# Attention steps of a hybrid decoder layer: value products issued in pairs, stride 1 ordered before stride 4, queries loaded four steps sooner

## The chip, the cores and the metric

The kernel runs on one core of one Trainium2 chip. The metric is the device time of one execution in microseconds, given as the median of several runs. TensorE is called PE here, VectorE DVE, ScalarE ACT, GpSimd POOL and SyncE SP, as in the profile. PE multiplies matrices, DVE and ACT work on rows in parallel, POOL does slower elementwise work, and nearly all DMA transfers of this kernel are issued by SP, one after the other in program order.

## What is computed

The layer projects 4096 prompt positions of width 1024 to queries, keys, values, an attention gate and a recurrent branch. Eight heads of width 64 evaluate three window patterns each: 128 keys back with stride 1, 4 and 16. Their outputs are merged by their softmax denominators, gated, joined with the recurrent branch and sent through one output projection with a layer norm. A short decode step (8 x 4 tokens) is computed beside it.

```python
DIL_PATTERNS = ((128, 1), (512, 4), (2048, 16))

def _dilated_prompt(q, k, v, d):          # one pattern, stride d
    l = s // d                            # d classes of l positions
    o, m, den = _band_attention(sub(q), sub(k), sub(v))   # window of 128 keys inside a class
    ...

def _merge(parts):
    m_max = jnp.max(jnp.stack([p[1] for p in parts]), axis=0)
    ws = [den * jnp.exp(m - m_max) for (_, m, den) in parts]
    total = sum(ws)
    return sum(w[..., None] * o for w, (o, _, _) in zip(ws, parts)) / total[..., None]

y_att = _merge([_dilated_prompt(qh, kh, vh, d) for _, d in DIL_PATTERNS])
```

## The kernel before

The kernel has four phases, one after the other. Phase 1 projects to queries, keys and values and writes them to scratch in HBM. Phase 2 is the attention of the prompt, and the change lies in it. Phases 3 and 4 are the recurrent branch, the decode step and the output projection.

**Units and steps.** Phase 2 runs through 8 units. A unit is one pair of heads (index `c`) and one half of the sequence (2048 positions, index `st`); units 0, 2, 4 and 7 have the first half, where part of the windows is empty and the step is smaller. A unit has 48 steps, so there are 384. A step handles 128 queries of two heads against 256 keys in one pattern (`pat` 0 is stride 16, 1 is stride 4, 2 is stride 1). Four steps (`b` = 0 to 3) form a group. In this kernel the groups of a unit come in the order (pattern, quarter): (1,0), (2,0), then the four groups of stride 16 on steps 8 to 23, then (1,1), (2,1), (1,2), (2,2), (1,3), (2,3). A quarter `nb` is 512 positions (`SPAN`).

**One step on the engines.** `front` (L510 on) issues four score products on PE (lines 515 and 516, tile `s`), adds the mask and takes the minimum on DVE (L522) and the exponential on ACT (L526). `middle` transposes the probabilities on PE (L535, tile `pt`) and copies them to SBUF (tile `pts`). `back` multiplies them with the values on PE (L551, tile `o`, two halves of 64 output partitions) and, at the last step of a group, copies the group's output to SBUF on ACT: tile `u16` for stride 16 (two buffers), tile `u1` for stride 4 (three buffers), tile `u2` for stride 1 (two). The loop at the end of phase 2 runs them as a pipeline: at step i it issues `front(i)`, then about four products of an independent gate projection (`feed`, tile `f`, lines 653 to 658), then `back(i-4)`, then `middle(i-2)`.

**Queries.** The queries of a unit lie in tile `QT`, in four quarters. Stride 1 reads them in place. For strides 4 and 16 POOL first gathers them (`gather_q`, L465, tile `qg`, four buffers), three steps ahead of the `front` that reads them. The stride 16 steps read all four quarters. A quarter of the next unit's queries is loaded (`load_Q`, L399, four transfers of 256 KB) two steps after the last step of that quarter.

**The merge.** When the last group of a quarter is done, at step L of the unit (L = 23, 31, 39, 47 for quarters 0 to 3), a chain of small pieces is put at fixed numbers of steps behind it: denominators out to HBM at L+3 and back at L+6, weights at L+11 and L+12 (store `wd<-wg`), `spread` at L+15 (two transfers `gb<-wd`, L607, 384 KB each), `combine` from L+17 and `store` at L+21 (`ad<-gb`, L623). `combine` is five POOL operations, the first at L620 and four at L798, one or two per step. All of it works in one tile `gb`, which has a single buffer, so `spread` of a quarter waits for `store` of the quarter before it. Quarter 2 of a unit is merged in steps 8 to 11 of the next unit and quarter 3 in steps 16 to 19.

**What sets the order.** Each engine and each queue works in program order. A POOL gather that stands behind an operation of `combine` in the program waits for it, and a transfer on SP that stands behind `store` waits until POOL has ended `combine`.

Of the kernel before, what the change touches and what calls it, by code (L numbers as in the profile page):

```python
# [8 lines left out]
F32 = mybir.dt.float32  # L9
# [14 lines left out]
SPAN = 512  # L24
# [6 lines left out]
class Kern:  # L31
# [373 lines left out]
    def phase2(self):  # L405
# [3 lines left out]
        def pool(name, bufs, space=None):  # L409
            return ctx.enter_context(tc.tile_pool(name=name, bufs=bufs, reuse_waits="tile", **({"space": space} if space else {})))  # L410
# [4 lines left out]
        up = pool("p2u", 3)  # L415
# [9 lines left out]
        KT, QT, Wg, load_K, load_Q = self.KT, self.QT, self.Wg, self.load_K, self.load_Q  # L425
# [26 lines left out]
        def defer(k, f, *a):  # L452
            later.setdefault(now[0] + k, []).append((f, a))
# [3 lines left out]
        def gather_q(x):  # L457
            x.q = qp.tile([128, 4, 128], F32R, tag="qg", name="qg")
            if x.pat:
                q = QT[:, x.a].rearrange("p h s (m r) -> p (h s) r m", r=4)[:, :, x.b]  # L460
                o = x.q
            else:
                q = QT.rearrange("p g h s (i r) -> p g (h s) r i", r=16)[:, :, :, 4 * x.a + x.b]
                o = x.q.rearrange("p k (g i) -> p g k i", g=4)
            nc.gpsimd.tensor_copy(o, q.bitcast(F32))  # L465
# [29 lines left out]
        def v_ap(c, st, pat, a, b, kb):  # L495
            g = st * 4 + a
            if pat == 0:
                return V16[c, st - 1 + kb, a][:, b]
            if pat == 1:
                return V4[c, g - 1 + kb][:, b]  # L500
            if kb:
                return V1[c, g][:, b]
            return V1[c, g][:, b - 1] if b else V1[c, g - 1][:, 3]
# [39 lines left out]
        def back(x):  # L543
            kbs = (0, 1) if x.full else (1,)
            if x.b == 0:
                x.grp.o = ps_o.tile([128, 512], F32, tag="o", name="o")
            o = x.grp.o
            for kb in kbs:
                v = v_ap(x.c, x.st, x.pat, x.a, x.b, kb)
                for h in range(2):  # L550
                    nc.tensor.matmul(o[h * 64:(h + 1) * 64, x.b * 128:(x.b + 1) * 128],  # L551
                                     v[:, h * 64:(h + 1) * 64], x.pt[:, h, kb],
                                     start=(kb == kbs[0]), stop=(kb == 1), skip_group_check=True)
            if x.b == 3:
                if x.pat == 0:
                    nc.scalar.copy(x.unit.u16.rearrange("p (i r) -> p r i", r=16)[:, 4 * x.a:4 * x.a + 4],
                                   o.rearrange("p (r i) -> p r i", r=4))
                else:
                    t = up.tile([128, SPAN], F32, tag=f"u{x.pat}", name="u", bufs=4 - x.pat)
                    if x.pat == 1:  # L560
                        nc.scalar.copy(t.rearrange("p (m r) -> p r m", r=4), o.rearrange("p (r m) -> p r m", r=4))
                    else:
                        nc.scalar.copy(t, o)
                    x.unit.u[x.pat, x.a] = t
# [46 lines left out]
        def combine(un, nb):  # L611
            s, gb = slice(nb * SPAN, (nb + 1) * SPAN), un.gb[nb]
            e = nc.gpsimd
            for k, (f, o, y) in enumerate(((e.tensor_mul, 0, un.u16[:, s]), (e.tensor_mul, 1, un.u[1, nb]),
                                           (e.tensor_mul, 2, un.u[2, nb]), (e.tensor_add, 0, gb[:, 1]),
                                           (e.tensor_add, 0, gb[:, 2]))):
                if k:
                    defer(min(k, 3), f, gb[:, o], gb[:, o], y)
                else:
                    f(gb[:, o], gb[:, o], y)  # L620
# [65 lines left out]
        def wx_stage(c):  # L686
            raw = wx[c] = (vp.tile([128, 512], F32, tag="v16", name="wst", bufs=4) if c < 4 else
                           vp.tile([128, 512], F32, tag=("v4", "v1")[c % 2], name="wst"))
            self.w_stage(raw, self.I["w_in"], DIN, 2048, c, True)
# [41 lines left out]
        units = []  # L731
        for i in range(8):
            un = S()
            un.i, un.c, un.st0, un.st, un.u, un.gb, un.w = i, i // 2, i % 2 if i < 6 else 7 - i, {}, {}, {}, {}
            units.append(un)
        steps = []
        for un in units:
            order = [(1, 0), (2, 0)] + [(0, w) for w in range(4)]
            for nb in range(1, 4):
                order += [(1, nb), (2, nb)]  # L740
            for pat, a in order:
                grp = S()
                for b in range(4):
                    x = S()
                    x.unit, x.c, x.st, x.pat, x.a, x.b, x.grp = un, un.c, un.st0, pat, a, b, grp
                    steps.append(x)

        def vload(i):
            x = steps[i]
            if x.b:  # L750
                return
            g = x.st * 4 + x.a
            if x.unit.i == 6 and x.a == 0 and x.pat:
                f = (load_V16, load_V4, load_V1)[x.pat]
                f(x.c, g - 1)
                return defer(5, f, x.c, g)
            if x.pat == 0:
                if x.st:
                    load_V16(x.c, 0, x.a)
                load_V16(x.c, x.st, x.a)  # L760
            elif x.pat == 1:
                load_V4(x.c, g)
            else:
                load_V1(x.c, g)

        vload(0)
        vload(4)
        for x in steps[:3]:
            gather_q(x)
        feed(self.f0[0])  # L770
        N, staged, split = len(steps), 0, 0
        for i in range(N + 26):
            now[0] = i
            if i < N:
                x = steps[i]
                un = x.unit
                if x.pat == 1 and x.a == 0 and x.b == 0:
                    un.u16 = u16p.tile([128, ST], F32, tag="u16", name="u16")
                    un.ac = sp.tile([128, 3, 16, 2, 2], F32, tag="ac", name="ac")
                    if un.i < 6 and un.st0 == 0:  # L780
                        defer(self.kl[0], load_K, un.c, 4, 2)
                        defer(self.kl[1], load_K, un.c, 6, 2)
                if x.pat and x.b == 0:
                    un.st[x.pat, x.a] = sp.tile([128, 4, 2, 2], F32, tag=f"st{x.pat}", name="st")
                x.stat = un.ac[:, 0, 4 * x.a + x.b] if x.pat == 0 else un.st[x.pat, x.a][:, x.b]
                front(x)
            feed(self.f0[i + 1] if i + 1 < len(self.f0) else self.fill_rate[x.unit.i] if i < N else 96)
            if 0 <= i - 4 < N:
                back(steps[i - 4])
            if 0 <= i - 2 < N:  # L790
                middle(steps[i - 2])
            if i + 3 < N and steps[i + 3].pat < 2:
                gather_q(steps[i + 3])
            for k in (1, 5):
                if i + k < N and (steps[i + k].pat == 0) == (k == 1):
                    vload(i + k)
            for f, a in later.pop(i, []):
                f(*a)  # L798
            if i >= self.wl[0] and staged < 8:
                wx_stage(staged)  # L800
                staged += 1
            if i >= self.wl[1] and credit[0] < -10 ** 8:
                for _ in range(self.wl[2]):
                    if split < staged:
                        wx_split(split)
                        split += 1
            if i < N and x.b == 3 and (x.pat == 2 and x.a or x.pat == 0 and x.a == 3):
                nb = x.a if x.pat else 0
                for d, f in zip(self.lag, (stats_out, stats_in, weights, weights_b, spread, combine)):
                    defer(d, f, un, nb)  # L810
                defer(24 if un.i == 7 and nb > 1 else 21, store, un, nb)
                if un.i + 1 < 8:
                    v = units[un.i + 1]
                    if nb == self.kl[4] and un.i % 2 and un.i < 6:
                        defer(self.kl[5], load_K, v.c, 0, 2)
                        defer(self.kl[6], load_K, v.c, 2, 2)
                    if nb and un.i == 5:
                        if nb < 3:
                            defer(self.kl[2], load_K, v.c, 3 + nb, 1)
                        else:  # L820
                            defer(self.kl[3], load_K, v.c, 6, 2)
                    defer(2, load_Q, v.c, v.st0, nb)
        assert split == 8
        while credit[0] > -10 ** 8 or later:
            now[0] += 1
# [842 lines left out]
```

## Time and profile before

| | us |
|---|---|
| median of 3 runs | 2411.47 |
| lowest and highest | 2410.02 and 2421.73 |
| the profiled execution | 2421.3 |
| its span, first to last instruction | 2419.3 |
| phase 2 in it, first score product to last value product | 592 to 1481 |

PE is busy for 2247.5 us of the span (93%), DVE 1476.3, ACT 1028.6 and POOL 860.5. In phase 2 the granted clock of PE is 0.91 to 1.00 of full speed in stretches of 100 us. The profile is read by a view of time (instructions of one engine in order, with the idle time before each and what ended it), by a view of waits, and by busy time in chosen stretches. Step n of unit u is the place of the (48u + n)th pair of L515 rows, counted from the first at 592.34 us.

### The profile page before, as it was taken

The page shows a single profiled execution, that of the slowest core. Times are in us where ns is not written, and L with a number is a line of the kernel's source. Part 1 is how long each engine was busy: PE and PEld are TensorE (multiplying, and loading weights), DVE is VectorE, ACT ScalarE, POOL GpSimd, SP SyncE. Part 2 cuts the span into 40 slices and gives each one's busy share as a digit, 9 for nine tenths or more (in the row PEclk, how much of TensorE's full clock was granted, in tenths as well). Part 3 has the DMA queues.
Part 4 walks back from the last instruction along what each step waited for, and adds up shares of the span by engine and source line. Part 5 has one row for each costly group of instructions (what it writes and reads, how often), then busy time and mean ns, then how long its engine had stood idle before and what let it go on. Part 6 is the DMA issues. An engine that isn't in the chain of part 4 may idle for free. (4 is left out here: it accounts for less than half of the span.)

```text
span 2419.3 us, 42698 instructions
## 1 busy us (share of the span) xinstructions
PE 2247.5 (93%) x15274; PEld 1890.9 (78%) x15274; DVE 1476.3 (61%) x3511; ACT 1028.6 (43%) x2691; POOL 860.5 (36%) x628
## 2 busy tenths in 40 slices
PE   6999999997999899979988988799999978989998
PEld 5878888886788778868777877799999956657776
DVE  4323222232576757646655655688999989998444
ACT  3212122222666566646655654455565632222221
POOL 1000000000445546464636465333333446656111
PEclk9999999998999999989999998899999999989999
DMA  6854556649676866777696755455545556668551
GB/s 173 257 189 153 174 174 200 209 186 245 181 171 169 203 158 174 181 181 172 161 203 173 172 143 137 154 171 153 162 157 176 193 176 226 239 223 324 204 187 57
DMA packets 324947, 444.18 MB, mean 184 GB/s; under 512 B 58629, under 2 KB 193413, under 8 KB 319617
## 3 DMA queue, kind: packets, MB, share of 16 engines
q1 hardware_dynamic: 324576, 440.94, 62.2%
q8 instruction: 122, 2.00, 0.4%
q14 instruction: 89, 0.72, 0.1%
q0 software_dynamic: 160, 0.52, 0.1%
HBM read 305.79 MB, written 135.60 MB: 182 GB/s over the span
## 5 line engine op out<-in xcount | busy, mean ns | idle before, releaser
L465 POOL CAST qg<-S 128x512 fp32r<-128x512 f32 x256 | 275.2, 1106 | 619.4 <-DMA S<-qd 482.6
L1280 PE MATMUL po<-S,mx 128*128 128x512 f32 x1536 | 377.5, 405 | 27.1 <-DVE xr L1334 17.1
L1280 PEld LDWEIGHTS po<-S,mx 128*128 128x128 f32 x1536 | 292.2, 192 | 118.3 <-issue 29.5
L522 DVE CUSTOM_DVE_ANT_0 sm<-s,mask 128x256 f32<-128x256 f32 (+1 forms) x768 | 270.8, 390 | 159.7 <-PE s L516 111.4
L526 ACT ACTIVATE sm<-sm,st 128x256 f32<-128x256 f32 (+1 forms) x512 | 251.7, 493 | 156.4 <-DVE st L522 130.4
L535 PE MATMUL pt<-ident,sm 128*128 128x128 f32 x1368 | 238.6, 292 | 11.1 <-ACT sm L526 10.9
L551 PE MATMUL o<-pts,v 128*64 128x128 f32 x2736 | 238.6, 290 | 7.6 <-DMA v<-vd 4.2
L539 DVE COPY pts<-pt 128x512 f32<-128x512 f32 x228 | 157.4, 690 | 138.5 <-PE pt L535 108.5
L515 PE MATMUL s<-S,qg 128*128 128x256 f32 x512 | 160.9, 334 | 54.2 <-POOL qg L465 53.1
L535 PEld LDWEIGHTS pt<-ident,sm 128*128 128x128 f32 x1368 | 144.9, 143 | 79.9 <-issue 55.5
L203 DVE TENSOR_TENSOR stg<-pp,stg 128x512 fp32r<-128x512 f32 x56 | 51.2, 917 | 238.7 <-ACT stg L202 234.1
L551 PEld LDWEIGHTS o<-pts,v 128*64 128x64 f32 x2736 | 143.9, 138 | 62.5 <-issue 3.6
L188 PE MATMUL pp<-S,xh 128*128 128x512 f32 x768 | 179.3, 394 | 6.4 <-ACT S L127 5.4
L314 PE MATMUL pp<-xh,S 128*128 128x512 f32 x448 | 176.0, 393 | 0.0
L188 PEld LDWEIGHTS pp<-S,xh 128*128 128x128 f32 x768 | 145.6, 190 | 38.5 <-ACT S L127 6.2
L315 PE MATMUL pp<-xh,S 128*128 128x512 f32 x448 | 174.5, 389 | 0.8 <-POOL xh L114 0.8
L316 PE MATMUL pp<-xh,S 128*128 128x512 f32 x448 | 174.6, 390 | 0.0
L526 ACT ACTIVATE sm<-sm,ac 128x128 f32<-128x128 f32 (+1 forms) x256 | 114.2, 447 | 109.5 <-DVE ac L522 109.2
L139 PE MATMUL xl<-xh,S 128*128 128x256 f32 x512 | 147.5, 288 | 8.9 <-DMA xh<-xtd 6.9
L143 PE MATMUL xl<-xh,S 128*128 128x256 f32 x512 | 147.7, 289 | 1.7 <-POOL S L128 1.3
L653 PE MATMUL f<-xh,S 128*128 128x256 f32 x512 | 147.3, 288 | 2.2 <-DMA xh<-xtd 2.1
L515 PEld LDWEIGHTS s<-S,qg 128*128 128x128 f32 x512 | 100.3, 196 | 62.5 <-POOL qg L465 59.9
(289 smaller groups left out, 5512.9 us busy)
## 6 DMA issues: line engine op xcount, KB each, us to landing
xh<-xtd SPq DMA_DIRECT2D x256, 256.0 KB, 5.4
S<-qd SPq DMA_DIRECT2D x128, 256.0 KB, 5.2
xtd<-xh SPq DMA_DIRECT2D x56, 512.0 KB, 2.6
gb<-wd SPq DMA_DIRECT2D x64, 384.0 KB, 6.2
v<-vd SPq DMA_DIRECT2D x264, 64.0 KB, 4.7
S<-kd SPq DMA_DIRECT2D x64, 256.0 KB, 7.2
xr<-in_x_prompt_dram SPq DMA_DIRECT2D x32, 512.0 KB, 4.8
arena<-in_cache_k_dram SPq DMA_DIRECT2D x16, 1024.0 KB, 9.0
```

The costliest lines, as they stand in the source:

```text
L188: nc.tensor.matmul(p, l, m, start=(c == 0 and a + b == 0), stop=(c == 7 and (a, b) == ((1, 0) if j < 2 else (0, 1))))
L314: nc.tensor.matmul(ps, wh, xh, start=(c == 0), stop=False)
L315: nc.tensor.matmul(ps, wh, xl, start=False, stop=False)
L316: nc.tensor.matmul(ps, wl, xh, start=False, stop=(c == 7))
L465: nc.gpsimd.tensor_copy(o, q.bitcast(F32))
L515: nc.tensor.matmul(s[:, h], q_ap(x, h, 0), k, start=True, stop=False)
L522: nc.vector.tensor_tensor_reduce(x.sm[:, h, o], s[:, h, i], self.mask[:, x.pat, o], -0.125, 3e38, ALU.add, ALU.min, x.stat[:, h, 0:1])
L526: nc.scalar.activation(x.sm[:, h, o], x.sm[:, h, o], AF.Exp, bias=x.stat[:, h, 0:1], scale=-1.0, accum_out=x.stat[:, h, 1:2])
L535: nc.tensor.transpose(p[:, h, kb], x.sm[:, h, kb * 128:(kb + 1) * 128], self.ident)
L539: e(x.pt, p)
L551: nc.tensor.matmul(o[h * 64:(h + 1) * 64, x.b * 128:(x.b + 1) * 128], v[:, h * 64:(h + 1) * 64], x.pt[:, h, kb], start=(kb == kbs[0]), sto ...
L1280: self.nc.tensor.matmul(ps[j], l, self.Wo[j][c][:, s], start=(c == 0 and s == 0 and l is mh), stop=(c == 7 and l is ml))
```

## The change

Five edits, all in phase 2:

- `back` is called at odd steps only, for two steps in a row: `back(i-5)` and `back(i-4)`. The products with the values of two steps so stand behind each other on PE.
- The order of a unit's groups has stride 1 ahead of stride 4 in each quarter: (2,0), (1,0), stride 16, then (2,1), (1,1) and so on. The last group of quarters 1 to 3 is now one whose queries POOL gathers.
- The tiles `u1` and `u2` exchange their numbers of buffers (two and three), and `combine` multiplies `u1` in its first operation and `u16` in its second.
- The first three gathers ahead of the loop are gone, since the first group needs none.
- `load_Q` for a quarter is issued one step after its last gather, which lies at L-3, instead of two steps after step L. It moves from L+2 to L-2.

```diff
-                    t = up.tile([128, SPAN], F32, tag=f"u{x.pat}", name="u", bufs=4 - x.pat)
+                    t = up.tile([128, SPAN], F32, tag=f"u{x.pat}", name="u", bufs=1 + x.pat)
...
-            for k, (f, o, y) in enumerate(((e.tensor_mul, 0, un.u16[:, s]), (e.tensor_mul, 1, un.u[1, nb]),
+            for k, (f, o, y) in enumerate(((e.tensor_mul, 1, un.u[1, nb]), (e.tensor_mul, 0, un.u16[:, s]),
...
-            order = [(1, 0), (2, 0)] + [(0, w) for w in range(4)]
+            order = [(2, 0), (1, 0)] + [(0, w) for w in range(4)]
             for nb in range(1, 4):
-                order += [(1, nb), (2, nb)]
+                order += [(2, nb), (1, nb)]
...
-        for x in steps[:3]:
-            gather_q(x)
...
-            if 0 <= i - 4 < N:
+            if 0 <= i - 4 < N and i % 2:
+                back(steps[i - 5])
                 back(steps[i - 4])
             if 0 <= i - 2 < N:
                 middle(steps[i - 2])
             if i + 3 < N and steps[i + 3].pat < 2:
-                gather_q(steps[i + 3])
+                y = steps[i + 3]
+                gather_q(y)
+                if y.b == 3 and (y.pat == 1 and y.a or y.pat == 0 and y.a == 3) and y.unit.i < 7:
+                    v = units[y.unit.i + 1]
+                    defer(1, load_Q, v.c, v.st0, y.a if y.pat else 0)
...
-            if i < N and x.b == 3 and (x.pat == 2 and x.a or x.pat == 0 and x.a == 3):
+            if i < N and x.b == 3 and (x.pat == 1 and x.a or x.pat == 0 and x.a == 3):
...
-                    defer(2, load_Q, v.c, v.st0, nb)
```

## Rows read from the trace of the kernel before

**Rows 1.** Page, busy time: us (share of the span) and instructions of each engine.
```profile
PE 2247.5 (93%) x15274; PEld 1890.9 (78%) x15274; DVE 1476.3 (61%) x3511; ACT 1028.6 (43%) x2691; POOL 860.5 (36%) x628
```

**Rows 2.** Busy time: stretch, length, PE, PEld, DVE, ACT, POOL, clock, DMA, GB/s.
```profile
942.00:971.00 29.00, 26.30 (x235) 21.57 (x235) 17.52 (x62) 16.70 (x53) 24.48 (x23) 1.00 0.52 145
971.00:997.00 26.00, 26.00 (x247) 22.23 (x244) 15.89 (x60) 18.62 (x59) 11.54 (x11) 1.00 0.75 178
```

**Rows 3.** Timeline of PE, one step with value products: start, us, operation, [idle<-releaser].
```profile
702.96 0.28 PE L656 MATMUL f<-xh,S 128*128 128x256 f32 x1
703.17 0.66 PE L551 MATMUL o<-pts,v 128*64 128x128 f32 x8
703.76 0.66 PE L535 MATMUL pt<-ident,sm 128*128 128x128 f32 x4
704.17 0.36 PE L515 MATMUL s<-S,qg 128*128 128x256 f32 x1
```

**Rows 4.** Timeline of PE: a step without value products, and a half step.
```profile
604.22 0.28 PE L658 MATMUL f<-xh,S 128*128 128x256 f32 x1
...
604.47 0.36 PE L515 MATMUL s<-S,qg 128*128 128x256 f32 x1
...
606.15 0.44 PE L551 MATMUL o<-pts,v 128*64 128x128 f32 x4 [0.27 <-DMA v<-vd]
606.52 0.44 PE L535 MATMUL pt<-ident,sm 128*128 128x128 f32 x2
```

**Rows 5.** Timeline of PE: first product of step 12 of unit 3.
```profile
942.32 0.39 PE L515 MATMUL s<-S,qg 128*128 128x256 f32 x1 [0.33 <-POOL qg L465]
```

**Rows 6.** Timeline of POOL: merges of unit 0 (quarters 0, 3), 2 (all), 6 (0, 3).
```profile
681.46 1.28 POOL L620 TENSOR_TENSOR gb<-gb,u 128x512 f32<-128x512 f32 x1 [10.31 <-ACT u L561]
...
740.32 1.28 POOL L620 TENSOR_TENSOR gb<-gb,u 128x512 f32<-128x512 f32 x1 [3.81 <-DMA gb<-wd]
...
902.14 1.28 POOL L620 TENSOR_TENSOR gb<-gb,u 128x512 f32<-128x512 f32 x1 [11.66 <-DMA v<-vd]
...
921.53 1.28 POOL L620 TENSOR_TENSOR gb<-gb,u 128x512 f32<-128x512 f32 x1 [8.66 <-DMA v<-vd]
...
925.26 2.64 POOL L798 TENSOR_TENSOR gb<-gb 128x512 f32<-128x512 f32 x2
...
939.98 1.29 POOL L620 TENSOR_TENSOR gb<-gb,u 128x512 f32<-128x512 f32 x1 [7.96 <-DMA v<-vd]
941.21 1.06 POOL L465 CAST qg<-S 128x512 fp32r<-128x512 f32 x1
...
946.81 2.64 POOL L798 TENSOR_TENSOR gb<-gb 128x512 f32<-128x512 f32 x2
...
958.89 1.28 POOL L620 TENSOR_TENSOR gb<-gb,u 128x512 f32<-128x512 f32 x1 [4.37 <-issue]
...
1358.63 1.29 POOL L620 TENSOR_TENSOR gb<-gb,u 128x512 f32<-128x512 f32 x1 [15.15 <-DMA v<-vd]
...
1412.24 1.27 POOL L620 TENSOR_TENSOR gb<-gb,u 128x512 f32<-128x512 f32 x1 [5.35 <-PE pt L535]
```

**Rows 7.** Timeline of the SP queue, merges of unit 2: start, us the issues took, transfer.
```profile
903.38 2.57 SPq L399 DMA_DIRECT2D S<-qd  x4
...
912.07 0.34 SPq L623 DMA_DIRECT2D ad<-gb  x1
...
914.85 1.24 SPq L607 DMA_DIRECT2D gb<-wd  x2
...
932.40 1.23 SPq L607 DMA_DIRECT2D gb<-wd  x2
```

**Rows 8.** Waits in phase 2: engine line <- releaser: us in total, times, longest.
```profile
ACT u L563 <- POOL gb L798: 73.1, 17, 6.6
PE s L515 <- POOL qg L465: 53.1, 23, 14.5
```

**Rows 9.** Timeline of POOL: first gathers of stride 16 in unit 6.
```profile
1276.14 4.05 POOL L465 CAST qg<-S 128x512 fp32r<-128x512 f32 x4 [7.60 <-DMA s4d<-st]
```

More of the change, by code (lines that the diff above doesn't have):

```diff
@@ L776, in phase2 @@
                 un = x.unit
-                if x.pat == 1 and x.a == 0 and x.b == 0:
+                if x.pat == 2 and x.a == 0 and x.b == 0:
                     un.u16 = u16p.tile([128, ST], F32, tag="u16", name="u16")
```

## Prediction, made before the changed kernel was run

> **What bounds the kernel now.** The page invites one answer: PE is busy 93% of the span [rows 1], so shorter work on PE should shorten the kernel. I read the rows stage by stage instead, since the change touches only phase 2. First the busy time of two stretches of twelve steps in unit 3 [rows 2]: steps 24 to 35 take 26.0 us with PE busy throughout, and steps 12 to 23, which hold the same number of steps, take 29.0 with PE busy 26.3 and POOL 24.5. PE sets the first, something else the second. Then PE's timeline at the head of the second stretch: step 12 waited for a gather [rows 5]. Then POOL's timeline [rows 6]: that gather stands right behind the first operation of the merge of quarter 2, at 939.98, which itself had idled 7.96 us for `gb<-wd`. Gather and score product follow at fixed distance: 939.98 to 942.32 is 2.3 us. Going through all units, steps 12 and 20 of units 1 to 7 (14 places) each start 2.3 us after the first operation of the merge of quarter 2 or 3. So in each unit PE is pinned twice to the merges, and what counts between two such places is the chain of merges, not PE.
>
> That chain is a ring, because `gb` has one buffer: `spread` is issued at 914.85 [rows 7], the merge begins 6.7 us later at 921.53, its last operation ends 6.4 us after that (925.26 + 2.64 = 927.90) [rows 6], `store` goes out, and only when it has landed can the next `spread` go (932.40). In unit 2 the four merges begin at 902.14, 921.53, 939.98 and 958.89: 19.4, 18.5 and 18.9 us apart, where eight steps at PE's own pace are 17.0. From the first to the fourth is 56.8 us; over the seven handovers from unit to unit (the first 681.46 to 740.32, the last 1358.63 to 1412.24 [rows 6]) the mean is 57.7. One period of a unit, step 20 to step 20, is then: L20 to the first merge, plus the three rings, plus 2.3. I cost the change on those links.
>
> **Products in pairs.** What the pair saves on PE: in a whole step the last gate product starts at 702.96 and the next step's scores at 704.17, 1.21 us [rows 3]. Without value products and with two transposes it is 604.22 to 604.47, 0.25 [rows 4]; two more transposes add 0.22 at 0.11 each, so 0.47. The block of eight records costs 1.21 - 0.47 = 0.74. Its inside is cheap: eight records from first to the transposes take 703.76 - 703.17 = 0.59, four take 606.52 - 606.15 = 0.37, so four more cost 0.22 and eight more 0.44. A second block right behind the first costs 0.44 instead of 0.74: 0.30 saved per pair, 0.15 per step, and 192 x 0.30 = 57.6 us if PE were on the path throughout. The rest is the price of changing between products of 64 and of 128 output columns: 0.21 from the last gate product to the first `o` [rows 3] against 0.12 between records of one kind. The Trainium skill (TensorEngine Tiling (Array Packing), Key Properties) says that a change of tiling mode drains the array; the rows agree, and by that page alone the whole 57.6 would be gained, which is rival A.
>
> How much of it is on the path: the steps between two pinned places that run ahead of the chain give their time back at the next pin. Only the pieces that follow PE's pace shorten a link. In "step 20 to first merge" these are the steps 24 to 38 (`spread` is placed at L+15 = 38): 14 x 0.15 = -2.1 us per unit.
>
> **The order of groups.** Now the part that speaks against it. Before, the gathers of (1,3) are for steps 40 to 43 and stand in the program at steps 37 to 40, ahead of the merge of quarter 0 (first operation at step 40); those of the next unit's (1,0) stand at 45 to 48, ahead of the merge of quarter 1 (step 48). After, stride 4 is second: the gathers of steps 44 to 47 stand at 41 to 44 and those of the next unit's steps 4 to 7 at 49 to 52, so both sit behind the first operation of a merge and between its others, just as stride 16 does today. Two things follow. PE gets two more pins, at steps 44 and 4 (before, a late merge held these places through ACT, which waited for `u2`: 73.1 us in 17 waits [rows 8]; the exchange of buffers and the new order inside `combine` remove that wait, and the gather takes its place at nearly the same distance, so I cost this at nothing). And the merges of quarters 0 and 1 get longer: with three gathers between the operations a merge takes 946.81 + 2.64 - 939.98 = 9.5 us, without 6.4 [rows 6]: +3.1 in the ring.
>
> **The loads of queries.** Each quarter's four transfers take SP 2.57 us to issue [rows 7]. Moving them from L+2 to L-2 puts quarter 2's (step 41 to 37) ahead of the `spread` of quarter 0 (38), and quarter 3's (49 to 45) ahead of the `spread` of quarter 1 (46). That costs `spread` from 0 (SP has a gap there) to 2.6 us of issue, and from 0 to about 3 more if 1 MB of queries moves ahead of it in the DMA queues. For quarter 0 I take half the issue, +1.3, because quarter 1's load leaves the same stretch (33 to 29). For quarter 1 I take the full 2.6 and +0.5: SP is held by `store` until POOL has ended, so nothing is issued early. The Trainium skill (DMA: Bandwidth & Descriptors, Queues, rings and completion order) says that descriptors are consumed in ring order on each DMA engine; no run here shows it for this pair of transfers. By it the full 3 us would stand in place of 0.5, and the total would be some 17 us higher.
>
> The gain of the earlier load is at one place: in unit 6 the first gathers of stride 16 idled 7.60 us [rows 9] for queries; I take -5 for it. Dropping the first gathers and ten pairs in unit 0 ahead of its first pin give -4. Unit 7 ends with steps 44 to 47 behind a merge (2.3 + 2.3 + 3.6 us pace instead of 2.0): +2 after its -0.8.
>
> **The sum.** Link to the first merge: -2.1 + 1.3 = -0.8. First ring (19.4 in unit 2): +3.1 for the gathers, -2.1 for the wait of `store` behind the merge's end, which the longer merge swallows (912.07 against 902.14 + 6.4 in unit 2, 3.5 us [rows 6, 7]; it is shorter in the later units, so I take three fifths), +2.6 + 0.5 for the queries: +4.1. Second ring: between +0.8 and +3.1, its gathers partly in the present slack; I take +1.5. Third ring: gathers in it already, 0. Together +4.8 per handover, x 7 = +33.6; with -5, -4 and +2: **+26.6 us**. Against the profiled execution's own time (2421.3) that is 2448; this execution lies 10 us above the median 2411.47, so the forecast is 2411.5 + 26.6 = **2438 us**. With all bounds low (-2.1, +0.5, +0.8 per handover) it is 2411.5 - 5.6 - 7 = 2399; with all high (+0.5, +6.6, +3.1) 2411.5 + 71.4 - 7 = 2476.
>
> **The rivals.** A, faster: PE's time is what counts. It decides if merges arrive ahead of the gathers behind them, that is if the ring falls under 8 x 1.98 = 15.8 us, or if the present rings are long because PE is slow (parts of the first ring follow PE's pace: `store` stood 3.5 us behind its merge). For it: the ACT wait goes, PE was busy 93%. Against: rings of 18.5 and 18.9 with the store on the heels of the merge. If the pace passes through at every link and nothing is added: -2.1 x 7 - 9 = 2388; with all 57.6 gained, 2354. B, a draw: the saved pace and the longer rings cancel, because the queries fall in gaps of SP and the gathers in the present slack: 2400 to 2422. C, the pairs don't come to stand as pairs: the second product waits for its `pts` copy, a switch is paid inside, nothing is saved on PE and the merges are lengthened all the same: +2.1 x 7 more, 2453.
>
> **Chances.** Forecast (2423 to 2466) 0.50, A 0.20, B 0.25, C 0.05. What a measurement of this kernel can tell from no change is about 0.5%, 12 us. Faster 0.20, same 0.25, slower 0.55. The range for 8 in 10 takes in B and the slower half of A, and the upper bound but for its last 10 us: 2390 to 2466; the forecast's own is 2423 to 2466.
>
> **What would show it.** After: `o` records in runs of 16, and runs from gate product to transposes without `o`, 0.12 apart, at the even steps; 24 steps between pins at 1.98 us instead of 2.13. On POOL the merges of quarters 0 and 1 with gathers between their operations, 9.5 us long; rings of 21 to 23, 20 and 20 us. PE's waits for `qg` above the present 53.1 us [rows 8], at steps 44 and 4, ACT's waits for POOL mostly gone, no gather in unit 6 waiting for queries. The prediction is wrong if the rings stay at 57.7 in sum or less, or if steps 44 and 4 start without waiting for a gather.

## Result and the profile after

The changed kernel takes 2491.64 us (median; 2490.79 to 2496.34) where the kernel before takes 2410.74 in the same comparison: a ratio of 1.0334, 95% interval 1.0313 to 1.0354, slower by 81 us. The forecast was 2438 (2390 to 2466): the sign was right, and the time lies 26 us above the range.

The loss lies in phase 2. From the start of its first score product to the start of its last row of L515 it took 881.9 us, now 955.7; it also starts 3.4 us sooner (589.0 in place of 592.3). Together that is +70.5, all of the 70.2 by which the two profiled spans differ (2489.5 and 2419.3). The other 11 of the 81 come from the anchor: the profiled execution of before lay that far above its own median.

The page's busy time (answers to [rows 1]): the instructions are as many as before, PE is busy 24 us less and ACT 5 us more. Only the weight loads (PEld), which overlap PE, grew by 28 us.

```profile
PE 2223.0 (89%) x15274; PEld 1918.6 (77%) x15274; DVE 1467.9 (59%) x3511; ACT 1033.8 (42%) x2691; POOL 857.6 (34%) x628
```

The waits of phase 2 (engine line <- releaser: us in total, times, longest; answers to [rows 8], 53.1 and 73.1 there):

```profile
PE s L515 <- POOL qg L465: 159.2, 62, 13.7
...
ACT u L561 <- POOL gb L620: 63.7, 17, 6.7
```

PE waits three times as long for gathers. Of the 159.2 us, 93.6 stand at steps 4 and 44, where the kernel before has none; of its 53.1, 14.5 was the very first step of the phase. ACT's wait for POOL has moved from `u2` to `u1` (L561 is the copy of stride 4) and is hardly shorter.

PE's timeline where it is not held, in unit 2 (answers to [rows 3]). The pairs are there: 16 records of `o` in a run, then a step with none, in which the transposes follow the last gate product after 0.12 us. Two steps take 898.57 - 894.61 = 3.96, so 1.98 each, as forecast.

```profile
893.17 1.09 PE L551 MATMUL o<-pts,v 128*64 128x128 f32 x16
894.19 0.66 PE L535 MATMUL pt<-ident,sm 128*128 128x128 f32 x4
894.61 0.37 PE L515 MATMUL s<-S,qg 128*128 128x256 f32 x1
...
895.52 0.28 PE L656 MATMUL f<-xh,S 128*128 128x256 f32 x1
895.64 0.60 PE L535 MATMUL pt<-ident,sm 128*128 128x128 f32 x4
896.00 0.37 PE L515 MATMUL s<-S,qg 128*128 128x256 f32 x1
...
898.57 0.36 PE L515 MATMUL s<-S,S 128*128 128x256 f32 x1
```

POOL's timeline over the merges of unit 2 (answers to [rows 6]). The merge of quarter 0 now has gathers between its operations and lasts 931.34 + 2.64 - 924.51 = 9.5 us, as forecast. The merges begin 23.2, 20.2 and 19.9 us apart (19.4, 18.5 and 18.9 before), and the first had waited for its `spread`.

```profile
924.51 1.26 POOL L620 TENSOR_TENSOR gb<-gb,u 128x512 f32<-128x512 f32 x1 [26.48 <-DMA gb<-wd]
925.71 1.08 POOL L465 CAST qg<-S 128x512 fp32r<-128x512 f32 x1
926.75 1.27 POOL L801 TENSOR_TENSOR gb<-gb,u 128x512 f32<-128x512 f32 x1
...
931.34 2.64 POOL L801 TENSOR_TENSOR gb<-gb 128x512 f32<-128x512 f32 x2
...
947.67 1.26 POOL L620 TENSOR_TENSOR gb<-gb,u 128x512 f32<-128x512 f32 x1 [12.62 <-DMA gb<-wd]
...
967.84 1.27 POOL L620 TENSOR_TENSOR gb<-gb,u 128x512 f32<-128x512 f32 x1 [5.52 <-DMA v<-vd]
...
987.78 1.28 POOL L620 TENSOR_TENSOR gb<-gb,u 128x512 f32<-128x512 f32 x1 [5.44 <-ACT pts L539]
```

PE at the same place: step 44 of unit 2 starts 926.85 - 924.51 = 2.3 us behind the merge's first operation.

```profile
926.85 0.58 PE L515 MATMUL s<-S,qg 128*128 128x256 f32 x1 [4.32 <-POOL qg L465]
927.22 0.41 PE L516 MATMUL s<-S,qg 128*128 128x256 f32 x1
927.44 0.41 PE L515 MATMUL s<-S,qg 128*128 128x256 f32 x1
```

The SP queue around both `spread`s (answers to [rows 7]):

```profile
909.72 0.53 SPq L599 DMA_DIRECT2D wd<-wg  x1
...
911.79 2.58 SPq L399 DMA_DIRECT2D S<-qd  x4
914.41 1.26 SPq L607 DMA_DIRECT2D gb<-wd  x2
...
934.00 0.33 SPq L623 DMA_DIRECT2D ad<-gb  x1
...
936.02 2.58 SPq L399 DMA_DIRECT2D S<-qd  x4
938.70 1.23 SPq L607 DMA_DIRECT2D gb<-wd  x2
```

Here is most of the loss in one picture. The weights go out at 909.72, and the four query transfers stand directly ahead of the `spread` that the merge waits for. They cost it 2.6 us of issue, and then it lands late: from issue to merge 924.51 - 914.41 = 10.1 us and 947.67 - 938.70 = 9.0, where before it was 6.7 [rows 6, 7].

Cut into the prediction's links, over the seven handovers (means in us, from the same rows in every unit: first score product of step 20, `wd<-wg`, first `gb<-wd`, first and last operation of the merge, `ad<-gb`):

| link | before | after | difference | forecast |
|---|---|---|---|---|
| step 20 to the weights' store | 38.1 | 36.1 | -2.0 | -2.1 |
| weights' store to `spread` | 4.3 | 7.9 | +3.6 | +1.3 |
| `spread` to first merge | 8.2 | 9.8 | +1.6 | 0 |
| **step 20 to first merge** | 50.5 | 53.8 | **+3.3** | **-0.8** |
| merge of quarter 0 | 6.4 | 9.5 | +3.1 | +3.1 |
| its end to `store` | 2.7 | 0.0 | -2.7 | -2.1 |
| `store` to `spread` | 2.8 | 4.5 | +1.7 | +2.6 |
| `spread` to second merge | 6.8 | 9.5 | +2.7 | +0.5 |
| **first ring** | 18.6 | 23.5 | **+4.9** | **+4.1** |
| **second ring** | 19.1 | 20.8 | **+1.6** | **+1.5** |
| **third ring** | 20.0 | 20.1 | **+0.1** | **0** |
| sum per handover | 108.3 | 118.2 | +9.9 | +4.8 |

Seven times 9.9 is 69.4; unit 7's end, from its step 20, adds 4.3 (59.7 to 64.0). Together that is phase 2's 73.9 but for 0.2.

### The profile page after: what moved, and what is told of

Read it like the earlier page. It is cut to its first block, busy times and chain, and to the rows that moved or that the text cites. A ratio compares the mean times of both kernels' runs of the same rounds, so it can differ in the third digit from the quotient of the medians.

```text
span 2489.5 us, 42662 instructions
## 1 busy us (share of the span) xinstructions
PE 2223.0 (89%) x15274; PEld 1918.6 (77%) x15274; DVE 1467.9 (59%) x3511; ACT 1033.8 (42%) x2691; POOL 857.6 (34%) x628
## 5 line engine op out<-in xcount | busy, mean ns | idle before, releaser
L465 POOL CAST qg<-S 128x512 fp32r<-128x512 f32 x256 | 275.8, 1098 | 575.5 <-DMA S<-qd 482.4
L515 PE MATMUL s<-S,qg 128*128 128x256 f32 x512 | 171.4, 353 | 159.6 <-POOL qg L465 159.2
L515 PEld LDWEIGHTS s<-S,qg 128*128 128x128 f32 x512 | 106.9, 209 | 177.9 <-POOL qg L465 177.5
L535 PE MATMUL pt<-ident,sm 128*128 128x128 f32 x1368 | 231.9, 289 | 0.3 <-DVE pts L539 0.3
L551 PE MATMUL o<-pts,v 128*64 128x128 f32 x2736 | 199.2, 287 | 2.1 <-DMA v<-vd 1.8
L535 PEld LDWEIGHTS pt<-ident,sm 128*128 128x128 f32 x1368 | 157.2, 144 | 34.2 <-ACT sm L526 17.8
L620 POOL TENSOR_TENSOR gb<-gb,u 128x512 f32<-128x512 f32 x32 | 40.9, 1277 | 395.0 <-DMA gb<-wd 242.5
L551 PEld LDWEIGHTS o<-pts,v 128*64 128x64 f32 x2736 | 151.5, 141 | 30.3 <-issue 3.9
L139 PE MATMUL xl<-xh,S 128*128 128x256 f32 x512 | 147.6, 288 | 10.4 <-DMA xh<-xtd 8.4
```

The lines of the kernel that those rows point to most:

```text
L515: nc.tensor.matmul(s[:, h], q_ap(x, h, 0), k, start=True, stop=False)
L535: nc.tensor.transpose(p[:, h, kb], x.sm[:, h, kb * 128:(kb + 1) * 128], self.ident)
```

## Experiments

Theory: the chain of merges sets the time, the order of groups and above all the place of the queries lengthen it, and the pairs give time only where a link follows PE's pace. Rivals: PE's pace is what counts, or the pairs themselves do the harm by bunching the products. Times of the experiments are ratios to the kernel before on the same chip (2417.95 us for the first four, 2419.63 for the others). Phase 2 is read from one profile of each. In the last three the lines below L465 stand one further down.

**The pairs alone.** On the kernel before:

```diff
-            if 0 <= i - 4 < N:
+            if 0 <= i - 4 < N and i % 2:
+                back(steps[i - 5])
                 back(steps[i - 4])
```

> Only the value products in pairs; order of groups, loads of queries and buffers as before. Theory (the ring of merges sets the period of a unit): PE's pace shortens the link from step 20 to the first merge by at most 2.1 us and the first ring by about 1, so 3 per handover, 7 handovers, and 4 in unit 0 ahead of its first pin: -25, about 2386 us; rings still 18 to 20. Rival A (PE sets the time, 192 pairs at 0.30): -57, 2354. Rival C (pairs save nothing on PE, or cost something): 2411 or more.

Measured: 2408.47, ratio 0.9961 (0.9946 to 0.9976), 9.5 us faster; phase 2 864.3, 17.5 less (the profiled execution of the kernel before is a long one, so the profiles differ by more than the medians). Twelve steps, 24 to 35, fell from 24.8 to 23.0 in the mean of the units, 1.8 = 6 x 0.30: the pair saves exactly what [rows 3, 4] said. But of the 57.6 that this makes over 192 pairs two thirds or more come back as waiting. The waits show where (before 53.1 in 23 [rows 8]):

```profile
PE s L515 <- POOL qg L465: 80.1, 36, 14.5
```

PE reaches the pins sooner and waits there. Rival A (-57) falls, and so does its weaker form in the prediction (-23): the interval ends at -13. My own -25, hardly apart from the latter, was also too much: link and first ring give 1.4 and 1.1 us per handover, the two other rings nothing.

**The queries two steps later.** On the changed kernel, so that the load comes at L, behind `spread`:

```diff
-                    defer(1, load_Q, v.c, v.st0, y.a if y.pat else 0)
+                    defer(3, load_Q, v.c, v.st0, y.a if y.pat else 0)
```

> The changed kernel with each quarter's load of queries issued two steps later, at L instead of L-2, so that it stands behind the spread of the earlier quarter (38, 46) and no longer ahead of it. Theory (the loads of queries ahead of the spread are the mis-sized term: in unit 2 the spread went out 2.9 us later after its weights and took 3.5 us longer to land): the link to the first merge falls by about 5 us and the first ring by about 3, 8 per handover, -56: about 2435. Rival (gathers behind the merges carry the whole loss, the place of the loads is indifferent): 2485 to 2495.

Measured: 2433.52, ratio 1.0058 (1.0040 to 1.0076), as the theory had it. This one number gives back 2.8% of the 3.3% lost. (The theory's 56 us came as 57.8 in phase 2 of the profiles and as some 67 by the ratios, which come from two chips.) The SP queue of this kernel in unit 2, and the two merges on POOL:

```profile
895.02 0.33 SPq L599 DMA_DIRECT2D wd<-wg  x1
...
896.87 1.25 SPq L607 DMA_DIRECT2D gb<-wd  x2
...
900.30 3.20 SPq L399 DMA_DIRECT2D S<-qd  x4
...
912.73 0.33 SPq L623 DMA_DIRECT2D ad<-gb  x1
...
914.83 1.84 SPq L607 DMA_DIRECT2D gb<-wd  x2
...
918.85 2.83 SPq L399 DMA_DIRECT2D S<-qd  x4
```

```profile
903.07 1.28 POOL L620 TENSOR_TENSOR gb<-gb,u 128x512 f32<-128x512 f32 x1 [18.66 <-DMA gb<-wd]
...
921.33 1.28 POOL L620 TENSOR_TENSOR gb<-gb,u 128x512 f32<-128x512 f32 x1 [7.55 <-DMA gb<-wd]
```

With the queries behind it, `spread` takes 6.2 and 6.5 us to the merge, and the first ring is 18.3 in place of 23.2, though its merge still has the gathers in it. Over all handovers the link falls from 53.8 to 49.0 and the first ring from 23.5 to 19.3, the second grows by 1.1; 8.0 x 7 = 56, and phase 2 fell by 57.8.

**The change without pairs.** On the changed kernel, `back` at every step as before:

```diff
-            if 0 <= i - 4 < N and i % 2:
-                back(steps[i - 5])
+            if 0 <= i - 4 < N:
                 back(steps[i - 4])
```

> The changed kernel with the value products issued step by step as before: new order of groups, early loads and buffers stay. Theory: the pairs give back only PE's pace in the link to the first merge, at most 2.1 us per handover and 4 at the start, so without them it is 5 to 20 us slower than the changed kernel: 2497 to 2512. Rival (the uneven steps that pairs make, about 1.4 and 2.6 us, are what hurts): faster than the changed kernel, toward 2411 to 2440.

Measured: 2499.27, ratio 1.0330 (1.0312 to 1.0349): the pairs are not the harm, and the rival falls. Beside the longer rings the pairs bring nothing that the ratios can show (1.0330 without them, 1.0334 with them), so the theory's 5 to 20 us are not confirmed by the times; phase 2 of the two profiles differs by 11 us, 966.5 to 955.7.

**The order alone.** The same, with the query load back at L+2:

```diff
-                if y.b == 3 and (y.pat == 1 and y.a or y.pat == 0 and y.a == 3) and y.unit.i < 7:
-                    v = units[y.unit.i + 1]
-                    defer(1, load_Q, v.c, v.st0, y.a if y.pat else 0)
...
+                    defer(2, load_Q, v.c, v.st0, nb)
```

> The new order of groups and the exchanged buffers alone: products step by step and loads of queries at L+2, both as before. Theory: two more merges get gathers between their operations, +1 to +2 in the first ring (its store has slack) and +1.5 in the second, nothing in the link: +15 to +30, 2425 to 2440. Rival (the order by itself carries the loss): 2480 or more. Rival (the order is harmless): 2405 to 2415.

Measured: 2444.10, ratio 1.0103 (1.0086 to 1.0119), 26 us, a little above what I expected. The merges of quarter 0 take 9.6 us here too, the first ring 19.7 and the second 22.2 (18.6 and 19.1 before): most of the price is in the second ring. The rows say why: both merges grew by 3.2, and `store` had stood 2.7 us behind the end of the first merge, which the longer merge could swallow, but only 0.9 behind the second. The exchange of buffers, the new order inside `combine` and the dropped first gathers are in this kernel too and were not run apart from the order. So single parts cost -9.5 (pairs), +26.2 (order, with these) and, between the last two kernels, +55.2 (queries); their sum of +72 stands against 81 for the whole, in which the gain of the pairs is lost.

**The gathers of stride 4 on another engine.** On the version with the queries later: if the merges lengthen because POOL gathers between their operations, and PE is held because gathers stand behind them, then DVE should free both.

```diff
-            nc.gpsimd.tensor_copy(o, q.bitcast(F32))
+            e = nc.vector if x.pat == 1 else nc.gpsimd
+            e.tensor_copy(o, q.bitcast(F32))
```

> The kernel with the later loads (pairs, stride 1 first, loads at L), and the gathers of stride 4 made by DVE instead of POOL. Theory (what is left of the loss, 16 us against the kernel before, is the gathers between the operations of the merges of quarters 0 and 1): merges of these quarters fall from 9.5 back to 6.4 us, first ring 19.3 to about 17, second 21.9 to about 19, 5 per handover, -35: 2390 to 2410. Rival (the rest of the loss is the exchange of buffers or the loads of values, or DVE has no room): 2428 or more.

Measured: 2426.96, ratio 1.0026 (1.0015 to 1.0038), faster than with POOL (1.0058) but between the two expectations. A miss. The merge of quarter 0 did shrink to 6.8 us; the time to `store` behind it grew back to 2.3 and the rings stayed at 18.5 and 21.0. PE's waits show a new one, on DVE, while the one for gathers fell from 116.4 us to 53.2:

```profile
PE s L516 <- POOL qg L466: 53.2, 34, 6.2
PE s L516 <- DVE st L523: 39.0, 27, 7.0
```

DVE works in order as well, and one place shows what holds it: weights that wait for the statistics' return, and behind them the minimum that frees PE's next score tile.

```profile
1017.89 0.28 DVE L586 TENSOR_REDUCE wm<-ac 32x32 f32<-32x96 f32 x1 [4.00 <-DMA ac<-s1d]
...
1019.32 0.58 PE L516 MATMUL s<-S,qg 128*128 128x256 f32 x1 [2.59 <-DVE st L523]
```

That this is the cause of the whole 39 us is argued from such places and was not tried. Whether the buffers or the loads of values hold a part of what is left stays open.

**Pairs, and the gathers that held PE before on DVE.** If the two old pins at steps 12 and 20 are what takes the pairs' gain, then moving the gathers of stride 16 for these steps should release it. On the kernel with pairs alone:

```diff
+            e = nc.vector if x.pat == 0 and x.a else nc.gpsimd
+            e.tensor_copy(o, q.bitcast(F32))
```

> Pairs alone (order, loads and buffers of the kernel before), and the gathers for steps 12 to 23 of each unit made by DVE instead of POOL, so that none stands behind a merge. Theory (PE is pinned at steps 12 and 20 by the gathers behind the merges): the pins go, the merge of quarter 2 falls from 9.4 to 6.4 us, PE runs on at its own pace until ACT's waits for u2 hold it: 35 to 70 below pairs alone, 2340 to 2375. Rival (DVE takes 96 x 0.6 = 58 us more and becomes the bound, or PE is held by something else): 2400 or more.

Measured: 2376.32, ratio 0.9823 (0.9805 to 0.9841): faster than both kernels by a clear margin, and just short of what I expected (some 33 us below pairs alone by the ratios, where 35 to 70 stood). The merge of quarter 2 falls from 9.4 to 6.9 us, the third ring from 20.2 to 18.9, and step 20 no longer follows the merge of quarter 3: its distance behind the first operation, 2.3 to 2.7 us in every unit before, is now between -4.9 and +3.1. PE's wait for gathers fell from 80.1 us in pairs alone to 28.6, of which 14.2 is the first step of the phase. At steps 12 to 23, where pairs alone had 59.7, none is left:

```profile
PE s L516 <- POOL qg L466: 28.6, 6, 14.2
```

**The multiplication that ACT waits for goes first.** On that version, `u2` ahead in `combine`:

```diff
-            for k, (f, o, y) in enumerate(((e.tensor_mul, 0, un.u16[:, s]), (e.tensor_mul, 1, un.u[1, nb]),
-                                           (e.tensor_mul, 2, un.u[2, nb]), (e.tensor_add, 0, gb[:, 1]),
+            for k, (f, o, y) in enumerate(((e.tensor_mul, 2, un.u[2, nb]), (e.tensor_mul, 1, un.u[1, nb]),
+                                           (e.tensor_mul, 0, un.u16[:, s]), (e.tensor_add, 0, gb[:, 1]),
```

> The same, and the merge multiplies u2 in its first operation instead of its third, so that ACT gets the buffer two operations earlier. Theory (with the gathers out of the way ACT's waits for u2 are the next hold): 5 to 20 below the run without it. Rival (ACT's waits lie beside other waits): no difference over 5 us.

Measured: 2374.43, ratio 0.9818 (0.9792 to 0.9844). ACT's wait for POOL fell from 73.2 us to 40.5, and the time did not move by anything that can be told: a miss.

```profile
ACT u L564 <- POOL gb L800: 73.2, 19, 8.8
ACT u L564 <- POOL gb L621: 40.5, 16, 7.4
```

(the run without it, then this one). Most of the 33 us of wait that went were off the path; the intervals, some 4 and 6 us to either side, leave room for the lower end of the theory.

## Where the prediction held and where it failed

**Bound by the merges: held.** Each of the seven handovers gives its loss in links and rings, and a change of two steps in the place of one load moves phase 2 by 58 us while PE's work stays the same. Two readings of the prediction were looser than it says: of its 14 places two start 2.7 and 3.0 us behind the merge, not 2.3, and the row of 939.98 names `v<-vd`, not `gb<-wd`, for the 7.96 us. The merge reads no `v`, and in unit 2 the first three merges begin 6.7, 6.7 and 7.6 us after their `spread`, so its reading stands. The pairs, 57.6 us of PE's work, moved 9.5. Rival A is out by the pairs alone, rival C by the steps of 1.98 us. Rival B has the conditions wrong: queries in gaps of SP is what the later load makes, and even then the order costs more than the pairs give (1.0058).

**Two new pins: held.** In the changed kernel steps 44 and 4 start 2.3 us behind the first operation of the merge, in every one of the 15 places; before, those steps began anywhere from 8.5 us ahead of that operation to 7.8 us behind it. Rings forecast at 21 to 23, 20 and 20 came as 23.5, 20.8 and 20.1, the merges at 9.5. That the second ring met its +1.5 (+1.6) is partly luck: it grew by 2.7 with the loads behind `spread` and by 3.1 with the order alone.

**ACT's wait gone: failed.** It is 63.7 us where it was 73.1, on `u1`. The order and the buffers did remove most of it, as forecast: it is 18.8 with the order alone and 18.5 with the loads two steps later. The early loads brought it back (57.5 with them and without pairs): with them the merges come later.

```profile
ACT u L561 <- POOL gb L620: 18.5, 9, 4.4
```

(the kernel with the queries two steps later). That it cost nothing in the sum, since PE is held by the gather at nearly the same distance, is argued; the last experiment shows for another kernel how little such a wait is worth.

**The step that failed: "-2.1 + 1.3 = -0.8" for step 20 to first merge.** Its first term was right (-2.0 to the weights' store). The second was wrong in two ways. I halved the issue of the queries because another load leaves the same stretch; but that load had stood elsewhere, not between the weights and `spread`, and the gap grew by 3.6, not 1.3: by more than the whole 2.6 of issue; the other 1.0 was not traced to one row. And I put the landing of `spread` behind 1 MB of queries into the bounds of the first ring, but not of this link, whose bound ended at +0.5: it is +1.6 here. The link came at +3.3, and 4.05 x 7 = 28 us of the gap between forecast and result are this step's. They alone carry 2438 to the upper end of the range.

**The term that was mis-sized: landing in the first ring, +0.5 taken, +2.7 measured.** The issue, 2.6 taken, was 1.7, and `store` gave 2.7 in place of 2.1, so the ring as a whole is only 0.8 off, which is luck. The merge began 6.8 us after the issue of the same `spread` before, 9.5 with the queries ahead of it and 6.9 with the queries behind it again. The delay of 9.5 - 6.8 = 2.7 us lies near the top of the range that the prediction gave it (0 to about 3), where 0.5 was taken. The Trainium skill (DMA: Bandwidth & Descriptors, Queues, rings and completion order) has descriptors consumed in ring order on each DMA engine. The two kernels that differ only in the place of these loads (9.5 and 6.9 us) agree with that rule, and the 3 us that the prediction set beside it was the better value.

**The rest.** The start came out: 3.4 us earlier and, net, no pace gained in the first 20 steps (47.7 to 47.5), -3.6 for -4. The changed kernel without pairs takes 50.8 there, so the pairs gave 3.4 and the new order took it back. In unit 6 the gathers of stride 16 no longer wait for queries, but its second ring fell only from 24.2 to 21.9, and that is inside the mean of +1.6 already: nothing of the -5 stands beside it. Unit 7 lost 4.3 for +2. So the gap of 54 us between 2438 and 2491.6 is 28 of the link, 6 of the first ring, 2 of the two others, 5 of unit 6, 2 of unit 7, half a us of the start, and 10 of the anchor: the 26.6 were added to the median, while the rows came from an execution 10 us above it, and the profiled execution of after did not lie above its median.

## What to carry to other kernels

Where engines and queues work in program order, find the places at which a fast engine is pinned to a chain behind a slow one, and cost a change on the links of that chain; work saved between two pins comes back as waiting until the pin is moved. When a load is moved earlier, look at each transfer that it passes: one that a chain waits for pays twice, once for the issue on the queue and once for landing behind the other's bytes. And a pin taken off one in-order engine can come back on the engine that takes the work, as PE's new wait for DVE suggests: moving gathers to DVE gave 1.4% at steps 12 to 23 and 0.3% at the steps of stride 4.

## What the runs showed of the hardware that was not expected

PE's clock fell where the pins held it. Busy time of two stretches of unit 2 in the changed kernel (stretch, length, PE, PEld, DVE, ACT, POOL, clock, DMA share, GB/s):

```profile
884.00:907.80 23.80, 23.80 (x234) 21.94 (x233) 16.08 (x63) 18.51 (x59) 7.09 (x7) 1.00 0.89 200
922.00:935.00 13.00, 8.68 (x56) 7.90 (x56) 5.38 (x18) 4.12 (x14) 10.41 (x9) 0.74 0.33 71
```

Full through steps 24 to 35, the granted clock is 0.74 on average where PE has just idled 4.3 us at the pin of step 44; there the records stand at 0.22 us from start to start (927.22 to 927.44, above), where 0.12 is usual, so part of the stretch ran at 1.2 GHz. From 620 to 1470 us the mean clock went from 0.97 to 0.92:

```profile
620.00:1470.00 850.00, 787.09 (x6949) 653.83 (x6947) 524.51 (x2030) 524.11 (x1744) 452.12 (x401) 0.97 0.72 173
```

```profile
620.00:1470.00 850.00, 700.72 (x6390) 626.05 (x6388) 473.46 (x1860) 482.64 (x1597) 407.70 (x363) 0.92 0.69 161
```

(the kernel before, then the changed one). How much of the time the clock itself costs was not separated: the version that beats both kernels has 0.95 in the same stretch and is faster all the same.

A gather of 128x512 values takes 0.63 us on DVE at either stride, and 1.07 to 1.14 on POOL (medians). The first two lines are from the version with stride 4 on DVE and stride 16 on POOL; the other two from pairs with most of stride 16 on DVE, where POOL has all of stride 4 and a quarter of stride 16. In the kernel before, all on POOL, the medians are 1.14 for stride 4 and 1.07 for stride 16.

```profile
L466 DVE CAST qg<-S x128: 604/630/1709, 597.1 to 1473.0; 128x512 fp32r<-128x512 f32 x128
L466 POOL CAST qg<-S x128: 1034/1072/1512, 604.6 to 1426.0; 128x512 fp32r<-128x512 f32 x128
...
L466 POOL CAST qg<-S x160: 1034/1134/1539, 590.5 to 1418.9; 128x512 fp32r<-128x512 f32 x160
...
L466 DVE CAST qg<-S x96: 594/633/1702, 624.4 to 1377.5; 128x512 fp32r<-128x512 f32 x96
```
